# Two heads' scores multiplied in turn, dilated attention by parity, and 22 projection products in halves

## The chip, the cores and the metric

The kernel runs on one core of a Trainium2 chip. The metric is the device time of one execution in microseconds (us), as the median of several runs.

## The reference, cut to what matters

Two stacks of layers over 256 tokens of width 1024, in FP32:

```python
def first_block(x, ...):                      # DEPTH = 2
    x = x + even_mixer(rmsnorm(x), ...)       # 8 stick-breaking heads, 8 NSA heads (2 KV groups)
    x = x + conv_glu_ffn(rmsnorm(x), ...)     # D_FF = 2816
    x = x + odd_mixer(rmsnorm(x), ...)        # 16 forgetting heads: softmax(q k / 8 + c_q - c_k) v
    x = x + conv_glu_ffn(rmsnorm(x), ...)
    return rmsnorm(x)

def second_block(x, ...):
    x = x + 0.5 * swiglu(rms(x));  x = x + hgrn2(rms(x));              x = x + 0.5 * swiglu(rms(x))
    x = x + 0.5 * swiglu(rms(x));  x = x + dilated_attention(rms(x));  x = x + 0.5 * swiglu(rms(x))
```

All heads of the attentions named here have 64 channels. Dilated attention has three groups (window and dilation 128 and 1, 512 and 4, 2048 and 16); a head's result is one softmax over the scores of the three groups, each with a bias by distance. NSA heads attend to compressed, selected and window keys; with 256 tokens the last two see all keys up to the query's own.

## The kernel before

The activations lie transposed in SBUF: channels on the 128 partitions in 8 chunks, 256 tokens along the free side (`x`, and its split into two FP32R parts `xH` and `xL`). Weights come from HBM in pieces of 1 MB (`w`, SP's queue), and ACT and DVE split each into `wH` and `wL` (L276, L277). A projection (`gemm`) makes 2 x 128 output channels for 256 tokens from such a piece: for each of 8 chunks `c` and two halves `j` three products of 256 columns, high by high (L323), then L326 and L327, 48 in all, accumulated in one PSUM bank (`ps_mm`). The products of the feed-forward output (L295 to L297) are of the same kind.

`gemm` has an argument `cut`: the first product of chunk 1 is then issued in several column pieces, with the same weights. Before, only feed-forward blocks use it: each of the six blocks (f0, f1, s00, s01, s10, s11) has five cut gate projections, at m = 4, 8, 12, 16 and 20, each block with the five patterns of `CUTS` in another rotation (L120). A block projects (0, g) and (0, u), computes the norm, which has a small product `ps_sm<-acc,ones` on PE, and goes on with (2, g), (2, u), (4, g) and so on. In s01 and s10 some extra work (bias table, a transpose) follows m = 8.

Attention heads lie in pairs: one 128-partition tile of `qT` and one of `kT` hold head a = 0 in partitions 0 to 63 and head a = 1 in partitions 64 to 127. Score products are FP32 with 64 contracted partitions and write to banks named `S` (two in the even mixer and the forgetting attention, three in the dilated attention); `mm` at L334 issues them and all other small products. DVE adds mask or bias and takes the maximum (L578, L580, L1340, L1344), ACT takes the exponent, PE transposes (L605, L1357), ACT copies, and PE multiplies with the values into `o`. In detail:

- `scores` (even and forgetting): one head and one bank a call. 128 late queries by 256 keys, then 128 early queries by 128 keys; in the forgetting attention each of the two is followed by an `extra` FP32R product that adds the decay (`CF`, `sel`).
- NSA `weigh(j, a)`: one head, both branches (selected, window); `mix(j, a)` multiplies with the values. `compressed` issues 16 products of 15 columns, in the order pair j, head a, query half tt.
- Forgetting `weigh`: head 0 in full, then head 1 in full.
- Dilated `weigh(u, G, bias, j, a, sm)`: one head, both parities t of the queries. Tokens stand with even and odd ones apart. Bank S0 takes group 0 of both parities (256 columns each), S1 groups 1 and 2 (128 columns each); DVE reads a half of a bank behind the products that fill it.

The order of the program is written by hand in strings (EVD, FXD, HGD, DLD; in DLD `q`, `k`, `v` are projections, `n` norms of heads, `t` their transposes, `w` a `weigh`, `m` a `mix`, and the digits are group of heads u, then g, or j and a). A list scheduler then orders each engine's instructions by that order and by what is ready, so projection products can stand between those of heads. PE works through its list in order.

Of the kernel before, what the change touches and what calls it, by code (L numbers as in the profile page):

```python
# [97 lines left out]
def _layout(parts):  # L98
    off, at = {}, 0
    for n, w in parts:  # L100
# [98 lines left out]
class Net:  # L199
# [106 lines left out]
    def gemm(self, out, W, by_token=False, X=None, w0=0, chunks=None, cut=None):  # L306
# [6 lines left out]
        for c in range(c0, c1):  # L313
            for j in range(2):
# [223 lines left out]
    def wout(self, tag, oH, oL, done):  # L538
# [18 lines left out]
    def scores(self, q, k, extra=None):  # L557

        S = self.psum((P, 384), "S")
        self.mm(S[:, 0:256], q[:, 128:256], k, stop=extra is None)  # L560
        if extra is not None:
            extra(S[:, 0:256], 256)
        self.mm(S[:, 256:384], q[:, 0:128], k[:, 0:128], stop=extra is None)
        if extra is not None:
            extra(S[:, 256:384], 128)
        return S

# [71 lines left out]
    def even(self, done):  # L639
        nc, tc = self.nc, self.tc  # L640
        with ExitStack() as ctx:
# [124 lines left out]
            def compressed(qr, kc, gview):  # L766

                Sc = [self.psum((P, 2, 4, 32), "S") for _ in range(2)]
                for j in range(4):
                    for a in range(2):  # L770
                        rows = slice(64 * a, 64 * a + 64)
                        for tt in range(2):
# [37 lines left out]
            def weigh(j, a):  # L810
                rows = slice(64 * a, 64 * a + 64)
                q = qr[j // 2][rows, j % 2, :]
                Sl = [self.scores(q, kkr[rows, b, :]) for b in range(2)]
                h = j + 4 * a
# [4 lines left out]
                nc.vector.tensor_mul(rs[:], rs[:], gview[:, :, h, 1:3])  # L819
                for b in range(2):  # L820
                    for tt in range(2):
                        v = ABs[b][1 - tt]
                        nc.vector.tensor_scalar(v, v, rs[:, tt, b:b + 1], None, ALU.mult)
                NS[j, a] = ABs

            def mix(j, a):
                if a == 0:
                    NO[0] = self.psum((P, 2, P), "o")
                o, ABs = NO[0], NS.pop((j, a))
                for b in range(2):  # L830
                    PT = self.transpose_p(ABs[b])
                    s = slice(128 * b + 64 * a, 128 * b + 64 * a + 64)
                    self.pv(o[:, :, 64 * a:64 * a + 64], vs[:, 0, s], vs[:, 1, s], PT, a + b == 0)
                if a == 0:
# [111 lines left out]
    def fox(self, done):  # L946
        nc, tc = self.nc, self.tc
        with ExitStack() as ctx:
# [40 lines left out]
            def weigh(u, j, qT, kT, e):  # L989
                Sl = []  # L990
                for a in range(2):
                    rows = slice(64 * a, 64 * a + 64)
                    h = 4 * u + 2 * j + a

                    def extra(S, n, h=h, rows=rows):
                        self.mm(S, sel[rows, h:h + 1].to_broadcast([64, P]), CF[rows, 0:n], start=False)
                    Sl.append(self.scores(qT[rows, j, :], kT[rows, j, :], extra))
# [248 lines left out]
    def dilated(self, kH, kL, Rkv, done):  # L1246
        nc, tc = self.nc, self.tc
        with ExitStack() as ctx:
# [9 lines left out]
            def project(u, g, n):  # L1258
                o = self.psum((P, 2, T))
                W = self.w("dl", n, u, g)  # L1260
                self.gemm(o, W, True, None if n == "q" else (kH, kL))
# [64 lines left out]
            def weigh(u, G, bias, j, a, sm):  # L1326
                rows = slice(64 * a, 64 * a + 64)
                hl = 2 * j + a
                q, k = ([G[g][i] for g in range(3)] for i in range(2))
                q, k = ([z[rows, j, :].rearrange("p (t n) -> p t n", t=2) for z in y] for y in (q, k))  # L1330
                S0, S1 = self.psum((P, 2, T), "S"), self.psum((P, 2, 2, P), "S")
# [264 lines left out]
```

## Time and profile before

| | |
|---|---|
| median of 3 runs | 1860.16 us (1859.75 to 1860.5) |
| profiled execution, its own time | 1861.3 us |
| its span, first to last instruction | 1859.5 us |
| busy: PE, PEld, DVE, ACT, POOL | 1841.7, 1806.4, 1270.9, 1042.1, 3.9 us |
| DMA | 314.72 MB, mean 169 GB/s |

Times in the profile are us from the first instruction. PE are products and transposes, PEld the loads of their stationary operand. Products overlap: the record of a 256-column product lasts some 0.28 us, while the next one starts earlier. The rows of the page and of the trace stand below.

### The profile page before, as it was taken

What the parts mean: (1) busy time and instruction counts of PE and PEld (TensorE: products, weight loads), DVE (VectorE), ACT (ScalarE), POOL (GpSimd) and SP (SyncE); (2) the same over time, 40 slices, a digit from 0 to 9 for tenths busy, and PEclk for the clock granted to TensorE, in tenths of its full rate; (3) what the DMA queues carried; (4) which work ended last, traced back from release to release, by engine and by line L of the source; (5) the groups of instructions that cost most, each with busy time, mean ns of one, the idle gap of its engine ahead of it and who ended that gap; (6) DMA issues with size and microseconds to landing.
All of it is one profiled execution on the core that took longest, in us unless ns stands there. A gap on an engine that the chain in (4) does not pass through costs nothing.

```text
span 1859.5 us, 37851 instructions
## 1 busy us (share of the span) xinstructions
PE 1841.7 (99%) x15729; PEld 1806.4 (97%) x15729; DVE 1270.9 (68%) x2695; ACT 1042.1 (56%) x2167; POOL 3.9 (0%) x18
## 2 busy tenths in 40 slices
PE   8999999999999999999999999999999999999999
PEld 7989999999999999999999999999999999999999
DVE  6557986654888686658998766766666456458763
ACT  5456665454666555546766545645456556556542
POOL 0000000000000000000000000000000000000000
PEclk9999999999999999999999999999999999999999
DMA  7313555531565546554335655555564344325553
GB/s 251 121 37 137 207 202 188 195 138 59 183 225 180 205 165 216 182 194 180 115 104 197 217 193 193 192 192 187 190 225 154 142 137 156 118 91 215 194 185 111
DMA packets 61160, 314.72 MB, mean 169 GB/s; under 512 B 10459, under 2 KB 21115, under 8 KB 28348
## 3 DMA queue, kind: packets, MB, share of 16 engines
q1 hardware_dynamic: 45792, 305.16, 46.5%
q10 hardware_dynamic: 15196, 7.15, 1.5%
q8 instruction: 123, 2.02, 0.4%
q14 instruction: 49, 0.40, 0.1%
HBM read 311.17 MB, written 1.11 MB: 168 GB/s over the span
## 4 chain that ended last, share of the span: by engine, by line
PE 93%; DVE 4%; DMA 2%; ACT 1%; issue 0%; ACTq 0%; SPq 0%
PE ps_mm L323 21%; PE ps_mm L326 21%; PE ps_mm L327 20%; PE ps_mm L297 6%; PE ps_mm L295 6%; PE ps_mm L296 6%; PE ps_S L334 5%; PE ps_o L334 4%; DVE wL L277 1%; DMA raw<-in_wall_dram 1%; PE ps_PT L1357 1%; PE ps_PT L334 1%; PE ps_PT L605 1%; DVE X L1165 0%; PE ps_PT L1302 0%; PE ps_PT L631 0%
## 5 line engine op out<-in xcount | busy, mean ns | idle before, releaser
L276 ACT CAST wH<-raw 128x512 fp32r<-128x512 f32 (+1 forms) x1212 | 651.6, 598 | 502.5 <-PE ps_mm L326 253.0
L277 DVE TENSOR_TENSOR wL<-raw,wH 128x512 fp32r<-128x512 f32 (+1 forms) x1212 | 754.8, 661 | 254.2 <-ACT wH L276 252.8
L323 PE MATMUL ps_mm<-xH,wH 128*128 128x256 f32 (+2 forms) x2602 | 716.0, 278 | 8.9 <-ACT xH L345 6.9
L326 PE MATMUL ps_mm<-xL,wH 128*128 128x256 f32 x2560 | 713.1, 279 | 0.6 <-DVE xL L346 0.3
L327 PE MATMUL ps_mm<-xH,wL 128*128 128x256 f32 x2560 | 712.4, 278 | 0.2 <-DVE wL L277 0.2
L323 PEld LDWEIGHTS ps_mm<-xH,wH 128*128 128x128 f32 x2602 | 487.4, 189 | 10.5 <-ACT xH L345 6.9
L327 PEld LDWEIGHTS ps_mm<-xH,wL 128*128 128x128 f32 x2560 | 482.8, 189 | 1.1 <-DVE wL L277 0.7
L326 PEld LDWEIGHTS ps_mm<-xL,wH 128*128 128x128 f32 x2560 | 482.2, 188 | 1.3 <-DVE xL L346 1.3
L297 PE MATMUL ps_mm<-hH,wL 128*128 128x256 f32 x1056 | 291.5, 276 | 0.0
L295 PE MATMUL ps_mm<-hH,wH 128*128 128x256 f32 x1056 | 291.5, 276 | 0.0
L296 PE MATMUL ps_mm<-hL,wH 128*128 128x256 f32 x1056 | 291.5, 276 | 0.0
L295 PEld LDWEIGHTS ps_mm<-hH,wH 128*128 128x128 f32 x1056 | 198.2, 188 | 0.0
L296 PEld LDWEIGHTS ps_mm<-hL,wH 128*128 128x128 f32 x1056 | 198.2, 188 | 0.0
L297 PEld LDWEIGHTS ps_mm<-hH,wL 128*128 128x128 f32 x1056 | 198.2, 188 | 0.0
L323 PE MATMUL ps_mm<-wH,kH 128*128 128x256 f32 x384 | 107.8, 281 | 0.0
L326 PE MATMUL ps_mm<-wL,kH 128*128 128x256 f32 x384 | 107.3, 280 | 0.0
L327 PE MATMUL ps_mm<-wH,kL 128*128 128x256 f32 x384 | 107.3, 279 | 0.0
L323 PE MATMUL ps_mm<-wH,xH 128*128 128x256 f32 x368 | 104.1, 283 | 0.0
L327 PE MATMUL ps_mm<-wH,xL 128*128 128x256 f32 x368 | 103.5, 281 | 0.0
L326 PE MATMUL ps_mm<-wL,xH 128*128 128x256 f32 x368 | 103.2, 280 | 0.0
L505 DVE TENSOR_TENSOR t<-ps_mm,R 128x512 f32<-128x512 f32 x66 | 45.5, 689 | 76.0 <-PE ps_mm L327 75.8
L323 PE MATMUL ps_mm<-oH,wH 128*128 128x256 f32 x256 | 72.8, 285 | 0.0
(296 smaller groups left out, 2264.5 us busy)
## 6 DMA issues: line engine op xcount, KB each, us to landing
raw<-in_wall_dram SPq DMA_DIRECT2D x254, 1024.0 KB, 4.8
raw<-in_wall_dram SPq DMA_DIRECT2D x40, 768.0 KB, 4.3
raw<-in_wall_dram SPq DMA_DIRECT2D x8, 512.0 KB, 3.3
bt<-scr ACTq DMA_DIRECT2D x8, 258.0 KB, 4.9
bt<-scr ACTq DMA_DIRECT2D x4, 512.0 KB, 6.4
x<-in_xin_dram SPq DMA_DIRECT2D x4, 256.0 KB, 5.6
raw<-in_wall_dram SPq DMA_DIRECT2D x4, 256.0 KB, 5.4
cw<-in_cmpw_dram ACTq DMA_DIRECT2D x1, 1024.0 KB
```

Of the source, the lines that this page charges most:

```text
L276: self.nc.scalar.copy(H[:, s], raw[:, s])
L277: self.nc.vector.tensor_sub(L[:, s], raw[:, s], H[:, s].bitcast(F32))
L295: nc.tensor.matmul(out, A[0], B[0], start=start, stop=False)
L296: nc.tensor.matmul(out, A[0], B[1], start=False, stop=False)
L297: nc.tensor.matmul(out, A[1], B[0], start=False, stop=stop)
L323: nc.tensor.matmul(out[:, j, at:at + n], A[0], B[0][:, at:at + n], start=c == c0 and j == 0, stop=False, **k)
L326: nc.tensor.matmul(out[:, j, :], A[0], B[1], start=False, stop=False, **k)
L327: nc.tensor.matmul(out[:, j, :], A[1], B[0], start=False, stop=c == c1 - 1, **k)
L334: self.nc.tensor.matmul(out, l, r, start=start, stop=stop, **k)
L505: nc.vector.tensor_mul(t2[:], u, Rb)
L605: nc.tensor.transpose(pp[:, i * P:(i + 1) * P], s, self.ident[:])
L1357: nc.tensor.transpose(pp[:, i], Pt[:, t, i * P:(i + 1) * P], self.ident[:])
```

## The change

Three things are edited; inputs, constants, layout of the weights and the number of score products stay.

1. `CUTS` and `CUT_OF` go. `cut` becomes a flag: the first product of the second chunk in two halves of 128 columns. It is set in each feed-forward block for (2, g), and in s01 and s10 for (10, u) too; in `wout` (the output projections of the four mixers) for m = 0; and in the dilated attention for ten projections (k00, q02, v02, q11, q20, q21, k22, k30, k31, v32), chosen by a rule on DLD: head work (`w`, `m`, `t`) came before, with only `n` or `s` between, and another projection, `n` or `s` comes next.
2. `scores` takes both heads of a pair and two banks, and issues the products of head 0 and head 1 in turn. NSA `weigh` and `mix` now go by branch b instead of by head a. In `compressed` the loops over a and tt are exchanged.
3. Dilated `weigh` and `mix` go by parity t instead of by head a: one call takes both heads of a pair for one parity, one bank per head, holding group 0 (256 columns), 1 and 2 (128 each), the products of the two heads in turn; DVE reads behind all six.

```diff
-CUTS = ((128, 128), (240, 16), (192, 64), (64, 64, 64, 64), (16, 240))
-CUT_OF = {t: {4 * (i + 1): CUTS[(i + k) % 5] for i in range(5)}
-          for k, t in enumerate(("f0", "f1", "s00", "s01", "s10", "s11"))}
...
-                for n in cut if cut and c == 1 and j == 0 else (T,):
+                for n in (P, P) if cut and c == c0 + 1 and j == 0 else (T,):
...
-                self.gemm(o, W, cut=CUT_OF[tag].get(m) if n == "g" else None)
+                self.gemm(o, W, cut=(m, n) in ((2, "g"), (10, "u") if extra else None))
...
-            self.gemm(o, W, X=(oH, oL), chunks=(0, k1))
+            self.gemm(o, W, X=(oH, oL), chunks=(0, k1), cut=m == 0)
...
+        S = [self.psum((P, 384), "S") for _ in range(2)]
+        for c, n, t in ((0, 256, slice(128, 256)), (256, 128, slice(0, 128))):
+            for a in range(2):
+                self.mm(S[a][:, c:c + n], q[a][:, t], k[a][:, 0:n], stop=extra is None)
+            for a in range(2):
+                if extra is not None:
+                    extra(a, S[a][:, c:c + n], n)
...
-            def weigh(j, a):
+            def weigh(j, b):
+                rows = [slice(64 * a, 64 * a + 64) for a in range(2)]
+                Sl = self.scores([qr[j // 2][r, j % 2, :] for r in rows], [kkr[r, b, :] for r in rows])
...
-                nc.vector.tensor_mul(rs[:], rs[:], gview[:, :, h, 1:3])
+                nc.vector.tensor_mul(rs[:], rs[:], gview[:, :, j::4, 1 + b])
...
-            def weigh(u, G, bias, j, a, sm):
+            def weigh(u, G, bias, j, t, sm):
+                S = [self.psum((P, 512), "S") for _ in range(2)]
+                for g, c, n in ((0, 0, 256), (1, 256, P), (2, 384, P)):
+                    for a in range(2):
+                        q, k = (G[g][i][64 * a:64 * a + 64, j, :] for i in range(2))
+                        self.mm(S[a][:, c:c + n], q[:, t * P:t * P + P], k if g == 0 else k[:, t * P:t * P + P])
...
+                for a in range(2):
+                    b0, b1 = bias[0][:, 2 * j + a, :], bias[1][:, 2 * j + a]
...
+                    for i, m in enumerate((m0, b1)):
+                        c = slice(256 * i, 256 * i + 256)
+                        nc.vector.tensor_tensor_reduce(two(Pt[:, a, c]), two(S[a][:, c]), m, 1.0, 2 * BIG, ALU.add,
+                                                       ALU.max, mx[:, a, i:i + 1])
...
+                cut = heads and its[min(i + 1, len(its) - 1)][0] in "qkvns"
+                heads = n in "wmt" or heads and n in "ns"
```

## Rows read from the trace of the kernel before

**Rows 1.** The page: the first row of part 1 (busy time of each engine, its share of the span, instructions), the row of the granted clock in part 2 (40 equal slices, in tenths), and the first row of part 4 (shares of the chain that ended last).

```profile
PE 1841.7 (99%) x15729; PEld 1806.4 (97%) x15729; DVE 1270.9 (68%) x2695; ACT 1042.1 (56%) x2167; POOL 3.9 (0%) x18
...
PEclk9999999999999999999999999999999999999999
...
PE 93%; DVE 4%; DMA 2%; ACT 1%; issue 0%; ACTq 0%; SPq 0%
```

**Rows 2.** Busy time in two stretches of 30 us in one feed-forward block, where the PE row of the timeline shows products of a projection alone. Columns: the stretch in us from the span's start, its length, then for PE, PEld, DVE, ACT and POOL the busy time and (x) the instructions that touch the stretch, the granted clock, the share of the DMA engines and GB/s. A product lasts 0.28 us by the profile and overlaps the next, so the spacing is (length + 0.28) / count.

```profile
676.00:706.00 30.00, 30.00 (x257) 30.00 (x256) 28.28 (x56) 17.99 (x33) 0.00 (x0) 1.00 0.51 184
...
711.00:741.00 30.00, 30.00 (x267) 30.00 (x266) 20.61 (x34) 14.32 (x27) 0.00 (x0) 1.00 0.50 178
```

**Rows 3.** Timeline of PE at four of the products that the kernel already does in pieces: start and length in us, engine, line, operation, names, shape, count. 194 us: two halves. 260 us: four quarters. 687 us: 192 and 64 columns. 1199 us: 16 and 240.

```profile
194.01 0.33 PE L323 MATMUL ps_mm<-xH,wH 128*128 128x128 f32 x2
...
194.35 0.28 PE L327 MATMUL ps_mm<-xH,wL 128*128 128x256 f32 x1
...
259.65 0.53 PE L323 MATMUL ps_mm<-xH,wH 128*128 128x64 f32 x4
...
260.22 0.28 PE L327 MATMUL ps_mm<-xH,wL 128*128 128x256 f32 x1
...
686.93 0.31 PE L323 MATMUL ps_mm<-xH,wH 128*128 128x192 f32 x2
...
1198.88 0.39 PE L323 MATMUL ps_mm<-xH,wH 128*128 128x16 f32 x2
```

**Rows 4.** Busy time in stretches of projections, columns as in rows 2. The first five lie in four feed-forward blocks (183: f0, 1002: s01, 1186 and 1223: s10, 1684: s11), the last three in the dilated attention.

```profile
183.00:193.00 10.00, 10.00 (x87) 10.00 (x87) 9.75 (x20) 7.79 (x15) 0.00 (x0) 1.00 0.38 140
...
1002.00:1014.00 12.00, 12.00 (x108) 12.00 (x107) 10.89 (x20) 9.14 (x17) 0.00 (x0) 1.00 0.63 221
...
1186.00:1216.00 30.00, 30.00 (x257) 30.00 (x256) 22.20 (x38) 17.01 (x31) 0.00 (x0) 1.00 0.58 203
...
1223.00:1231.00 8.00, 8.00 (x73) 8.00 (x72) 5.58 (x9) 3.44 (x7) 0.00 (x0) 1.00 0.34 131
...
1684.00:1697.00 13.00, 13.00 (x113) 13.00 (x112) 9.76 (x18) 8.55 (x15) 0.00 (x0) 1.00 0.62 231
...
1398.00:1408.00 10.00, 10.00 (x88) 10.00 (x87) 6.06 (x11) 6.23 (x12) 0.00 (x0) 1.00 0.51 184
...
1452.00:1482.00 30.00, 30.00 (x257) 30.00 (x256) 15.61 (x30) 15.12 (x31) 0.00 (x0) 1.00 0.44 160
...
1484.00:1499.00 15.00, 15.00 (x130) 15.00 (x129) 11.53 (x24) 8.82 (x19) 0.00 (x0) 1.00 0.47 166
```

**Rows 5.** Timeline of PE at two stretches of score products of the dilated attention that stand between other work, each with the row that follows it. [...]

```profile
1427.95 0.70 PE L334 MATMUL ps_S<-k,qT 64*128 64x256 f32 x2
...
1428.58 0.55 PE L334 MATMUL ps_o<-vN,PT 128*128 128x64 f32 x3
...
1436.39 0.71 PE L334 MATMUL ps_S<-k,qT 64*128 64x128 f32 x4
...
1437.02 0.39 PE L327 MATMUL ps_mm<-wH,xL 128*128 128x256 f32 x1
```

**Rows 6.** Timeline of PE in the even mixer where score products of the stick-breaking heads (qT,kT) and of the NSA heads (kkr,nqr) follow one another.

```profile
106.83 0.48 PE L334 MATMUL ps_S<-kkr,nqr 64*128 64x256 f32 x1
...
106.94 0.38 PE L334 MATMUL ps_S<-qT,kT 64*128 64x128 f32 x2
...
107.15 0.38 PE L334 MATMUL ps_S<-kkr,nqr 64*128 64x256 f32 x1
...
107.16 0.27 PE L334 MATMUL ps_S<-qT,kT 64*128 64x128 f32 x1
...
107.37 0.38 PE L334 MATMUL ps_S<-kkr,nqr 64*128 64x128 f32 x2
```

**Rows 7.** Busy time of the instructions that write or read the score banks ps_S alone (columns as in rows 2, POOL left out by the view): the NSA heads of the even mixer with some of the stick-breaking ones, the forgetting attention, the dilated attention.

```profile
105.00:146.00 41.00, 16.81 (x87) 11.80 (x84) 11.40 (x37) 0.98 (x2) 1.00 0.06 21
...
389.00:453.00 64.00, 15.48 (x96) 11.76 (x96) 8.75 (x28) 0.00 (x0) 1.00 0.26 90
...
1421.00:1647.00 226.00, 32.50 (x192) 22.50 (x192) 26.06 (x64) 0.00 (x0) 1.00 0.38 131
```

**Rows 8.** Timeline of PE: the first and the last of the 28 stretches of score products in the dilated attention.

```profile
1421.83 3.19 PE L334 MATMUL ps_S<-k,qT 64*128 64x256 f32 x20
...
1644.84 0.48 PE L334 MATMUL ps_S<-k,qT 64*128 64x128 f32 x2
```

**Rows 9.** Timeline of PE in the forgetting attention: the start of a pair of heads whose products are not interrupted and the row after its end (the rows between are left out), and a first product that stands alone between transposes and value products.

```profile
389.30 0.70 PE L334 MATMUL ps_S<-kT,qT 64*128 64x256 f32 x2
...
390.86 0.39 PE L323 MATMUL ps_mm<-xH,wH 128*128 128x256 f32 x1
...
404.74 0.70 PE L334 MATMUL ps_S<-kT,qT 64*128 64x256 f32 x2
```

**Rows 10.** Timeline of PE: one of the four stretches of score products with the compressed keys (15 columns).

```profile
97.91 1.06 PE L334 MATMUL ps_S<-kcr,nqr 64*128 64x15 f32 x8
```

**Rows 11.** The first head stage of the dilated attention: the reduction that empties half a score bank and the read of its accumulator (groups of instructions: line, engine, operation, names, shapes, count, busy us, mean ns of one, idle us before, releaser), and the busy time of the stage (columns as in rows 2).

```profile
L1340 DVE CUSTOM_DVE_ANT_1 Pt<-ps_S,bt 128x256 f32<-128x256 f32 x8 | 3.3, 421 | 4.7 <-PE ps_S L334 4.2 <-PE ps_PT L1357 0.5
...
L1340 DVE DVE_READ_ACCUMULATOR2_ANT mx<- 128x1 f32 x8 | 0.7, 83 | 0.0
...
1421.00:1450.50 29.50, 29.38 (x233) 26.53 (x232) 16.07 (x60) 19.59 (x43) 0.00 (x0) 1.00 0.35 107
```

More of the change, by code (lines that the diff above doesn't have):

```diff
@@ L304, in gemm_a, with gemm @@
             self.mm3(out, (W[0][:, c, s], W[1][:, c, s]), (XH[:, c, :], XL[:, c, :]), c == 0, c == KC - 1)
-    def gemm(self, out, W, by_token=False, X=None, w0=0, chunks=None, cut=None):
+    def gemm(self, out, W, by_token=False, X=None, w0=0, chunks=None, cut=False):
         nc = self.nc
@@ L769, in compressed @@
                 for j in range(4):
-                    for a in range(2):
-                        rows = slice(64 * a, 64 * a + 64)
-                        for tt in range(2):
+                    for tt in range(2):
+                        for a in range(2):
+                            rows = slice(64 * a, 64 * a + 64)
                             self.mm(Sc[a][:, tt, j, 0:15], qr[j // 2][rows, j % 2, tt * P:(tt + 1) * P], kc[rows, :])
@@ L989, in weigh, with extra @@
             def weigh(u, j, qT, kT, e):
-                Sl = []
-                for a in range(2):
-                    rows = slice(64 * a, 64 * a + 64)
+                rows = [slice(64 * a, 64 * a + 64) for a in range(2)]
+                def extra(a, S, n):
                     h = 4 * u + 2 * j + a
-                    def extra(S, n, h=h, rows=rows):
-                        self.mm(S, sel[rows, h:h + 1].to_broadcast([64, P]), CF[rows, 0:n], start=False)
-                    Sl.append(self.scores(qT[rows, j, :], kT[rows, j, :], extra))
+                    self.mm(S, sel[rows[a], h:h + 1].to_broadcast([64, P]), CF[rows[a], 0:n], start=False)
+                Sl = self.scores([qT[r, j, :] for r in rows], [kT[r, j, :] for r in rows], extra)
                 sm = self.sp.tile([P, 2, 2], F32, name="sm2")
@@ L1256, in dilated, with project @@
             RS = cp.tile([P, 2, 2], F32, name="RS")
-            def project(u, g, n):
+            def project(u, g, n, cut):
                 o = self.psum((P, 2, T))
                 W = self.w("dl", n, u, g)
-                self.gemm(o, W, True, None if n == "q" else (kH, kL))
+                self.gemm(o, W, True, None if n == "q" else (kH, kL), cut=cut)
                 return o
@@ L1324, in biases @@
                 return b0, b1
-            def weigh(u, G, bias, j, a, sm):
[L1327 to L1331, printed above, removed]
-                b0, b1 = bias[0][:, hl, :], bias[1][:, hl]
+            def weigh(u, G, bias, j, t, sm):
+                two = lambda z: z.rearrange("p (b n) -> p b n", b=2)
+                S = [self.psum((P, 512), "S") for _ in range(2)]
+                for g, c, n in ((0, 0, 256), (1, 256, P), (2, 384, P)):
+                    for a in range(2):
+                        q, k = (G[g][i][64 * a:64 * a + 64, j, :] for i in range(2))
+                        self.mm(S[a][:, c:c + n], q[:, t * P:t * P + P], k if g == 0 else k[:, t * P:t * P + P])
@@ L1346, in weigh @@
                 nm = self.sp.tile([P, 2], F32, name="nmj")
                 nc.vector.tensor_reduce(nm[:], mx[:], AX.X, ALU.max, negate=True)
-                for t in range(2):
-                    nc.scalar.activation(Pt[:, t], Pt[:, t], AF.Exp, bias=nm[:, t:t + 1], accum_out=sm[:, t, a:a + 1])
-                return Pt
-            def mix(v, Pt, j, a, o):
-                s = slice((2 * j + a) * 64, (2 * j + a) * 64 + 64)
-                for t in range(2):
+                for a in range(2):
+                    nc.scalar.activation(Pt[:, a], Pt[:, a], AF.Exp, bias=nm[:, a:a + 1], accum_out=sm[:, t, a:a + 1])
@@ L1355, in mix @@
+                return Pt
+            def mix(v, Pt, j, t, o):
+                for a in range(2):
+                    s = slice((2 * j + a) * 64, (2 * j + a) * 64 + 64)
                     pp = self.psum((P, 4, P), "PT")
                     for i in range(4):
-                        nc.tensor.transpose(pp[:, i], Pt[:, t, i * P:(i + 1) * P], self.ident[:])
+                        nc.tensor.transpose(pp[:, i], Pt[:, a, i * P:(i + 1) * P], self.ident[:])
                     PT = ap.tile([P, 4, P], F32, name="PT", bufs=3)
@@ L1364, in dilated @@
             B = {}
-            for it in DLD.split():
+            its, heads = DLD.split(), True
+            for i, it in enumerate(its):
                 n, w = it[0], tuple(int(z) for z in it[1:])
+                cut = heads and its[min(i + 1, len(its) - 1)][0] in "qkvns"
+                heads = n in "wmt" or heads and n in "ns"
                 if n == "q" or n == "k":
-                    B[(n,) + w] = project(*w, n)
+                    B[(n,) + w] = project(*w, n, cut)
                     if it[2:] == "0" and n == "k":
@@ L1371, in dilated @@
                 elif n == "v":
-                    B[("v",) + w] = values(project(*w, n))
+                    B[("v",) + w] = values(project(*w, n, cut))
                 elif n == "s":
```

54 lines of the change are left out of this document (17 added, 37 removed).

## The prediction

> **What bounds the kernel now.** I read the page first. TensorE has work under way for 99% of the span, its clock is granted at the full level in every slice, and 93% of the chain that ended last is PE, nearly all of it the three product lines of the projections [rows 1]. DVE is at 68% and ACT at 56%, so they are covered on average. The kernel ends earlier only if PE's own stream of instructions gets shorter. A busy share of 99% cannot say how fast that stream runs, because products overlap in the record; so the second thing to read is the spacing of product starts. In one block, the same 256-column product starts every (30 + 0.28) / 257 = 0.1178 us in one stretch and every 30.28 / 267 = 0.1134 us in another [rows 2]. Both stretches are busy for all of their 30 us at clock 1.00, so this is no wait and no throttle: there are two paces, 4.4 ns apart, and the reader should see that only the counts differ.
>
> Third, I read what happens at the products that are already cut [rows 3], and which pace holds around them [rows 4]; last the score products of the heads, their spacing alone and beside others [rows 5 to 10], and DVE behind them [rows 11]. The profiled execution took 1861.3 us for a span of 1859.5; the median of the runs is 1860.16, so terms taken from the span can be subtracted from the median as they stand.
>
> **Part 1: the halves.** A cut into two pieces takes from 194.01 to the next-but-one product at 194.35, 0.34 us where two products at the fast pace take 0.227: it costs 0.114. A cut in four takes 0.57 and costs 0.34 [rows 3]. The old list has 30 cut products, five in each of six blocks; in each block four are in two pieces and one in four. Removing them gives 24 x 0.114 + 6 x 0.34 = 4.8 us. The new 22 (six at (2, g), two at (10, u), four in the output projections, ten in the dilated attention) cost 22 x 0.114 = 2.5 us. Net **-2.3 us**.
>
> What a cut does to the pace: before the two halves at 194.01 the pace is 10.28 / 87 = 0.118, and in s10 the slow pace (257 in 30 us) runs through the cut 16 + 240 at 1198.88 and ends at the next one, two halves at 1221.6, behind which 73 in 8 us is 0.1134. The cut 192 + 64 at 686.93 lies inside the slow stretch of rows 2 and changes nothing either [rows 2 to 4]. The third pair of halves that met the slow pace, in s11, also ended it. So two halves set the fast pace in three cases of three, and two other patterns failed once each. I take halves as sure.
>
> Feed-forward: in f0, f1 and s11 the slow pace holds from the small product of the norm to the cut in (4, g), and the new cut in (2, g) lies 96 products earlier: 3 x 96 x 4.4 ns = 1.27 us. In s00 and s10 the first old cut failed, so the new one is 288 products earlier: 2 x 288 x 4.4 ns = 2.53 us. s01 is at 12.28 / 108 = 0.1137 already [rows 4] and gains nothing. Sum **-3.8 us**.
>
> Dilated attention: from 1398 on almost every projection is slow (88 in 10 us, 257 in 30, 130 in 15) [rows 4]. A cut helps to the next interruption, since the transposes and head products set the pace anew. Where the cut projection starts behind transposes and runs undisturbed, the products behind the seventh count: q02 and v02 90 each, q20 and k22 138 each, k30 42, v32 90, together 588 x 4.4 ns = **-2.6 us**. Those of q11, q21 and k31 stand among head products in PE's order of before, and long slow stretches such as the one at 1452 begin behind that head work; I give them nothing, up to 2.3 us if the order changes (518 products). The output projections: 36-product pieces chopped by head work, 0 (0 to 0.3). In the two blocks with extra work, (10, u) stands where the pace is fast already: 0. Part 1 is **-8.7 us**, from -5 (dilated gains nothing) to -11.
>
> **Part 2: scores in turn.** No product is added or removed; the two heads of a pair stand in partitions 0 to 63 and 64 to 127, and the order decides whether neighbours differ in that. Alone, two records of 256 columns take 0.63 us to the next row and four of 128 take 0.63: with 0.216 and 0.112 a record this leaves 0.19 for entering and leaving such a stretch [rows 5]. When the two kinds of heads stand side by side, the trace shows two streams at once: records of kkr at 106.83, 107.15 and 107.37 keep their own spacing while three of qT,kT start between them, one 10 ns behind a kkr record [rows 6]. So adjacent products of different halves run at the same time. The Trainium skill states this too (TensorE: Matmul & The Clock Gate, Part 3, "The mechanism": tiles in different row groups overlap, starting some 4 ns apart); the trace agrees where the two are neighbours, and by its span model every pair would cost one product, the case of rival (a) below.
>
> Price of the pairs. Dilated: each of 16 weighs (4 groups, 2 pairs, 2 parities) issues 2 x (2 x 0.216 + 4 x 0.112) = 1.76 us, paired 0.88. All paired saves 14.1 us. But the records now take 32.5 us busy [rows 7], while 64 x 0.216 + 128 x 0.112 + 28 x (0.19 + 0.07) = 35.5 (0.07 is the modelled tail of each of the 28 stretches [rows 8]); so 3 us overlap already and must be taken off. The second parity of a pair finds one free score bank of three; the other comes free only when DVE has read two halves at 0.50 us each [rows 11]. Meanwhile a scheduler that takes what is ready puts the first head's three products in alone, as it did with lone products in before. I pair all first parities and a quarter of the second, 10 of 16: 8.8 us less most of the 3, that is **-6.5** (-4 to -11).
>
> Forgetting attention: an uninterrupted pair takes 1.56 us [rows 9]; one head by its prices takes 2 x 0.216 + 2 x 0.112 + 0.11 + 0.06 + 0.19 = 1.02, so 0.54 is saved. Three of the eight pairs run like this now, by the timeline: 1.6 us is the low end. If all eight take 1.02 and a tail, 15.48 busy [rows 7] becomes 8.7, 6.8 saved. The others start with a lone product in a hole [rows 9]; I take the middle, **-3.7**. NSA heads: 32 x (0.216 + 0.112) = 10.5 us of records, at best 5.2 saved, nothing if two banks never come free together; **-2.6**. Compressed keys: 32 records of 0.112, eight to a stretch [rows 10]; 1.8 or 0, **-0.9**. Sum -13.7.
>
> What is late next: per weigh, DVE's four reductions take 2.0 us and follow the products; they started between them before, now all of one bank's products come first. In the head stage DVE is busy 16.1 and ACT 19.6 of 29.5 us [rows 11], and projection products stand there to fill holes, so most of it stays covered; I take a tenth off for new waits: **-12.3 us**. Everything else (exponents, transposes, value products, the gates' strided slices) keeps its count and size: nothing.
>
> Sum: 1860.2 - 8.7 - 12.3 = **1839 us**.
>
> **Rivals.** (a) *All pairs meet*: scores -11.1 - 6.8 - 5.2 - 1.8 = -24.9, with the halves 1827. For it: the clean overlap of rows 6. Against: the score banks. (b) *Pairs are torn or eaten*: a bank wait or a filler stands between the two heads nearly everywhere, each extra stretch costs 0.19, or what PE gains it waits for DVE; only the halves count, 1851.5. For it: 28 stretches for 16 weighs now [rows 8]. The Trainium skill has a rule for this (TensorEngine Tiling, "Key Properties": a change of tiling mode drains the engine); the 0.19 of rows 5 agrees. (c) *The halves don't hold*: the pace behind them comes out slow, or head work resets it at once; 2.3 of the 8.7 remain, 1845.5. (d) *Slower*: PE works in order, and the second head's first product now stands ahead of the first head's rest. If in each of the 32 weighs it waits for the bank while DVE reads two halves, 32 x 1.0 = 32 us are lost against 21 gained: 1871. It decides from 0.66 us per weigh. Against: PE is busy for 29.4 of 29.5 us in a head stage [rows 11], so such holes are filled with other products now, and all its idle time is 18 us [rows 1].
>
> **Numbers.** Forecast 0.55, (a) 0.18, (b) 0.15, (c) 0.05, (d) 0.03; 0.04 for gains and waits that cancel. A change of under 0.2% (3.7 us) can't be told from none here. (a), (b), (c) and the forecast are all over it: faster 0.93, same 0.03, slower 0.04. The range takes in (a) and (b), 1826 to 1852; the forecast's own is 1831 to 1846.
>
> **What would show it.** Halves: at most a few cut products at 0.34 us, and behind (2, g) in every block about 267 products in 30 us; in the dilated attention 0.1134 behind q02, v02, q20, k22. Pairs: four 256-column records in some 0.55 us; busy time of ps_S near 26 us instead of 32.5 in the dilated attention, near 12 instead of 15.5 in the forgetting attention. Wrong if ps_S stays near 32 and 15 (b), if PE shows waits on DVE mx of more than 10 us in all (d), or if stretches behind two halves still count 257 (c).

## The result and the profile after

The changed kernel takes **1847.4 us** (1846.3 to 1848.3), the kernel before 1859.95: a ratio of 0.9934, interval 0.9917 to 0.9951, 12.6 us less. A second comparison gave 1849.0 against 1861.0, again 0.9934 (0.992 to 0.9947). The forecast was 1839, with a range of 1826 to 1852 and a narrower one of its own, 1831 to 1846. Sign and wide range held; the narrow range was missed by 1.4 us, and the point was 8 us too low.

The page after, same parts as [rows 1]: TensorE is as full as before, with 20 product records fewer, and the chain is more PE's than before.

```profile
PE 1826.5 (99%) x15709; PEld 1792.6 (97%) x15709; DVE 1268.5 (69%) x2695; ACT 1041.6 (56%) x2167; POOL 3.9 (0%) x18
...
PEclk9999999999999999999999999999999999999999
...
PE 95%; DVE 2%; ACT 1%; DMA 1%; issue 0%; SPq 0%; ACTq 0%
```

Busy time in stretches of projections, columns as in [rows 2]. The first four lie behind the new halves of (2, g) in f0, s00, s10 and s11; the next two behind the halves of q02 and v02 in the dilated attention, then a long stretch behind head work there, then two behind the halves of q20 and k22.

```profile
184.00:214.00 30.00, 30.00 (x267) 30.00 (x267) 26.50 (x49) 19.76 (x36) 0.00 (x0) 1.00 0.55 182
...
672.00:702.00 30.00, 30.00 (x267) 30.00 (x266) 27.70 (x53) 16.99 (x30) 0.00 (x0) 1.00 0.53 187
...
1182.00:1212.00 30.00, 30.00 (x268) 30.00 (x267) 23.01 (x37) 17.62 (x31) 0.00 (x0) 1.00 0.55 194
...
1676.00:1706.00 30.00, 30.00 (x267) 30.00 (x266) 25.04 (x41) 18.83 (x34) 0.00 (x0) 1.00 0.62 222
1390.00:1400.00 10.00, 10.00 (x87) 10.00 (x86) 5.84 (x11) 5.71 (x13) 0.00 (x0) 1.00 0.40 149
1402.00:1411.00 9.00, 9.00 (x78) 9.00 (x78) 6.08 (x10) 5.49 (x12) 0.00 (x0) 1.00 0.52 186
1441.00:1471.00 30.00, 30.00 (x267) 30.00 (x266) 17.20 (x34) 15.93 (x33) 0.00 (x0) 1.00 0.48 176
1475.00:1489.00 14.00, 14.00 (x121) 14.00 (x121) 11.23 (x24) 8.04 (x17) 0.00 (x0) 1.00 0.45 152
1535.00:1549.00 14.00, 14.00 (x121) 14.00 (x120) 10.23 (x22) 9.02 (x19) 0.00 (x0) 1.00 0.45 170
```

The feed-forward blocks count 267 or 268 in 30 us where [rows 2, 4] had 257 before a cut took effect. In f0, s00 and s10 the slow pace held up to the new halves and ended there; in s11 this execution was fast a little ahead of them. In the dilated attention the new halves don't set it: 9.28 / 78 = 0.119 and 14.28 / 121 = 0.118 us a product is the slow pace, behind four cuts. The one fast stretch shown there (1441) begins behind head work and no cut.

Score products. Each leaves two records in the trace (192 records for the 96 products of the dilated attention). First the busy time of ps_S alone, as in [rows 7]: forgetting attention 15.48 to 11.91, dilated attention 32.50 to 28.14.

```profile
387.00:450.00 63.00, 11.91 (x96) 8.39 (x96) 8.37 (x28) 0.00 (x0) 1.00 0.27 93
1412.00:1634.00 222.00, 28.14 (x192) 19.86 (x192) 24.14 (x64) 0.00 (x0) 1.00 0.39 133
```

Then PE's timeline after: a compressed stretch, a forgetting pair and the row behind it, the first weighs of the dilated attention.

```profile
100.21 1.06 PE L332 MATMUL ps_S<-kcr,nqr 64*128 64x15 f32 x8
...
387.93 0.70 PE L332 MATMUL ps_S<-kT,qT 64*128 64x256 f32 x4
388.28 0.47 PE L332 MATMUL ps_S<-CF,selr 64*128 64x256 f32 x2
388.59 0.39 PE L332 MATMUL ps_S<-kT,qT 64*128 64x128 f32 x4
388.73 0.31 PE L332 MATMUL ps_S<-CF,selr 64*128 64x128 f32 x2
388.96 0.39 PE L321 MATMUL ps_mm<-xH,wH 128*128 128x256 f32 x1
...
1413.30 2.40 PE L332 MATMUL ps_S<-k,qT 64*128 64x256 f32 x18
1415.64 0.39 PE L321 MATMUL ps_mm<-wH,xH 128*128 128x256 f32 x1
1415.86 0.28 PE L324 MATMUL ps_mm<-wL,xH 128*128 128x256 f32 x1
1416.36 0.89 PE L332 MATMUL ps_S<-k,qT 64*128 64x256 f32 x4 [0.22 <-DVE mx L1338]
```

A forgetting pair takes 388.96 - 387.93 = 1.03 us; it was 1.56 [rows 9]. The compressed stretch is what it was (1.06 us for eight records, [rows 10]). The 18 records at 1413 are the first weigh with its heads in turn (the records of the two heads start 7 ns apart) and, behind it, all of one head's products of the second weigh: they take 2.34 us. The other head's products wait at 1416 for DVE to empty a bank.

What PE waited for, by the view of waits (total us, times, longest):

```profile
PE ps_sm L332 <- DVE rel L1400: 2.3, 1, 2.3
...
PE ps_S L332 <- DVE mx L1338: 1.1, 4, 0.4
PE ps_o L332 <- ACT PT L606: 0.5, 1, 0.5
```

All three are new. The first stands at the start of s01, the others belong to the heads and are small.

### The profile page after: what moved, and what is told of

It reads as the page before. It is cut to its first block, busy times and chain, and to the rows that moved or that the text cites. A ratio compares the mean times of both kernels' runs of the same rounds, so it can differ in the third digit from the quotient of the medians.

```text
span 1846.5 us, 37819 instructions
## 1 busy us (share of the span) xinstructions
PE 1826.5 (99%) x15709; PEld 1792.6 (97%) x15709; DVE 1268.5 (69%) x2695; ACT 1041.6 (56%) x2167; POOL 3.9 (0%) x18
## 4 chain that ended last, share of the span: by engine, by line
PE 95%; DVE 2%; ACT 1%; DMA 1%; issue 0%; SPq 0%; ACTq 0%
PE ps_mm L321 21%; PE ps_mm L324 21%; PE ps_mm L325 21%; PE ps_mm L293 6%; PE ps_mm L292 6%; PE ps_mm L294 6%; PE ps_S L332 4%; PE ps_o L332 4%; DMA raw<-in_wall_dram 1%; PE ps_PT L1351 1%; DVE wL L274 1%; PE ps_PT L332 1%; PE ps_PT L604 0%; PE ps_PT L1298 0%; ACT wH L273 0%; PE ps_PT L630 0%
## 5 line engine op out<-in xcount | busy, mean ns | idle before, releaser
L321 PE MATMUL ps_mm<-xH,wH 128*128 128x256 f32 x2568 | 713.1, 278 | 8.8 <-ACT xH L343 7.0
L321 PE MATMUL ps_mm<-wH,kH 128*128 128x256 f32 (+1 forms) x390 | 108.1, 279 | 0.0
L321 PE MATMUL ps_mm<-wH,xH 128*128 128x256 f32 (+1 forms) x372 | 104.2, 282 | 0.0
L321 PEld LDWEIGHTS ps_mm<-wH,kH 128*128 128x128 f32 x390 | 72.9, 188 | 0.0
```

## The experiments

**The halves alone.** The kernel before with the new cuts and its old heads:

```diff
-    for n in cut if cut and c == 1 and j == 0 else (T,):
+    for n in (P, P) if cut and c == c0 + 1 and j == 0 else (T,):
...
```

> The kernel before with the 22 halves in place of its 30 old cuts, scores and order of heads as before. Theory: halves set the fast pace only where the weights are stationary (feed-forward, output projections); in the dilated attention, where the activations are stationary, they only cost 0.114 us each. Feed-forward -8.5 us, dilated +1.1: 1852.5 us, and behind q02, v02, q20, k22, k30, v32 the spacing stays 0.1177 before and after the cut. Rival (the prediction's step): the halves also act in the dilated attention, another -2.6 and more: 1849, spacing 0.1133 behind these cuts.

Measured: 1856.6 against 1860.1, ratio 0.9982 (0.9973 to 0.9991): 3.5 us, less than either theory. Part of it is the clock at the opening (below): at a granted clock of 0.999 over the span the two executions took 1854.5 and 1854.7, those of the kernel before 1860.1 to 1861.6. In the profiles the opening up to the NSA scores is 2.6 us longer than before. The six feed-forward blocks are together 6.7 us shorter, where the theory had 8.5; s01 gains nothing, because PE waits 1.4 us there (the last experiments show for what). In the dilated attention the stretches that begin with a half-cut projection or behind head work count as before:

```profile
1450.00:1480.00 30.00, 30.00 (x257) 30.00 (x256) 15.62 (x30) 15.11 (x31) 0.00 (x0) 1.00 0.47 159
1483.00:1497.00 14.00, 14.00 (x121) 14.00 (x120) 11.19 (x24) 8.00 (x17) 0.00 (x0) 1.00 0.50 160
```

The dilated stage with its output projection takes 316.7 us, against 315.8 before: ten cuts are paid for and nothing comes back. Rival (c) of the prediction, that halves don't hold, is true for this stage and false for the feed-forward.

**The scores alone.** The changed kernel with the old list of 30 cuts.

> The changed kernel with the 30 old cuts in place of the 22 halves, so the new order of scores alone. Theory: the score products give 10 us of PE (2.5 NSA, 3.4 forgetting, 4.2 dilated), waits for the score banks take about 1.5 back: 1851.5 us, or 1849.5 if the long stretch of projections behind the first head stage of the dilated attention comes out at the fast pace again without any halves. Rival: half of what PE gains is lost to new waits: 1855.

Measured: 1852.6, ratio 0.9954 (0.9939 to 0.9969), 7.5 us. The two parts alone add up to 11.0, the whole is 12.6 and, measured again below, 12.0: no large interaction.

**No cut at all.**

```diff
-    self.gemm(o, W, cut=CUT_OF[tag].get(m) if n == "g" else None)
+    self.gemm(o, W)
```

> The kernel before with no product cut. Theory: a pace holds until something interrupts the products; without a cut the five feed-forward blocks that start slow stay slow to their end, some 1500 products each: +29 us for the pace, -4.8 for the cuts saved: 1884 us. Rival: the pace comes right by itself within a block: 1855 us.

Measured: 1881.6 (1873.8 to 1886.0), ratio 1.0107 (1.008 to 1.0133). The pace lasts until something ends it. Stretches of f0, s00 and f1 without a cut:

```profile
185.00:215.00 30.00, 30.00 (x257) 30.00 (x256) 27.17 (x50) 20.44 (x37) 0.00 (x0) 1.00 0.51 185
760.00:790.00 30.00, 30.00 (x257) 30.00 (x256) 21.01 (x35) 15.26 (x30) 0.00 (x0) 1.00 0.50 178
500.00:530.00 30.00, 30.00 (x267) 30.00 (x266) 27.03 (x50) 20.34 (x37) 0.00 (x0) 1.00 0.55 201
```

f0 and s00 are slow here, f1 is fast. In this execution f0, s00 and s11 stay slow to their ends, the output included (62.07 us instead of 59.73); s10 is fast behind the extra work that follows m = 8, s01 and f1 without a cut. f1 was slow up to the small product of the norm and fast behind it, so such a product can change the pace too.

**A bank of its own for each head.** In the dilated attention head 0 takes the single bank of one name, head 1 one of two of another, and the six products are chained in turn (the lines of the chain are left out here):

```diff
-    self.banks(ctx, mm=2, S=3, PT=2, o=1)
+    self.banks(ctx, mm=2, S=1, Sb=2, PT=2, o=1)
...
-    S = [self.psum((P, 512), "S") for _ in range(2)]
+    S = [self.psum((P, 512), "S"), self.psum((P, 512), "Sb")]
...
```

> The changed kernel; in the dilated attention head 0 of a pair always takes one bank of its own and head 1 the other two in turn, and the six products are tied in order, so that none starts before the bank that comes free last. Theory: the score banks tear the pairs (head 0's three products go ahead alone); now 12 of 16 calls have all their products side by side: busy time of ps_S in the dilated attention falls from some 28.7 us to 24, the median by 3 to 4 us, to 1843.5. Rival: the pairs meet, but PE then waits for DVE or ACT instead: ps_S falls, the time stays at 1846 to 1848.

Measured: 1851.9 (1848.1 to 1855.5), ratio 0.9958 (0.9941 to 0.9975): no gain. From the first record of each stretch to the start of what follows, summed over the stage by the timeline, score products took 31.2 us before, 27.0 in the changed kernel and 24.3 here: in twelve of the sixteen weighs the two heads now run side by side. But the stage as a whole takes 317.1 us instead of 312.7. PE's waits in it are now:

```profile
PE ps_PT L1357 <- ACT Pt L1349: 1.8, 5, 0.4
PE ps_S L1330 <- DVE mx L1344: 1.6, 3, 0.7
```

3.4 us against 1.1. Projection products are also slow more often: of the starts in the stage 1327 followed at the slow pace instead of 917, 410 x 4.4 ns = 1.8 us. These two make 4.1 of the 7.1 us that were lost beside the scores (4.4 more for the stage, 2.7 less for the scores). The other 3 us are not located; projection products now break the score stretches more often, 33 stretches instead of 24. Banks and chain came in one edit, so what each of them did is not separated.

**The changed kernel again.**

> The changed kernel unaltered, beside the next two. The first comparison gave 0.9934 (12.6 us less). If the gain is the sum of the two parts run alone (3.5 us for the halves, 7.5 us for the scores), its ratio comes out at 0.994 or a little above, 11 us less; if the two help each other, as a forecast of 21 us had it, it is 0.992 or less. At the same granted clock the halves alone were 5.5 us ahead of the kernel before, so 13 us are expected at the same granted clock.

Measured: 0.9934 (0.992 to 0.9947), 12.0 us: the sum of the parts within what can be told.

**No halves in the dilated attention.**

```diff
-    self.gemm(o, W, True, None if n == "q" else (kH, kL), cut=cut)
+    self.gemm(o, W, True, None if n == "q" else (kH, kL))
```

> The changed kernel, but the ten projections of the dilated stage are not cut. Theory: with the activations as the stationary operand the halves set no pace, they only cost 0.113 us each, so this kernel is 1.1 us faster than the changed one (0.0006 of the time), and the stretches at q02, v02, q20, k22, k30 and v32 count at 0.1178 us per product in both. Rival: the halves are what let the three long fast stretches of the dilated stage come about (558 products of 4.4 ns, 2.5 us), so leaving them out costs 2.5 - 1.1 = 1.4 us.

Measured: 1846.0, ratio 0.9916 (0.9903 to 0.993); beside it the changed kernel had 1849.0. The dilated stage is 1.06 us shorter than in the first profile of the changed kernel (311.6 against 312.7), as the theory has it, but only 0.4 us shorter than in the second, where the stretch behind k22 came out fast. The rival is half right: the stretches at 1516 and 1641, fast with the halves in both profiles, are slow without them (1198 slow starts against 917 and some 780). (With the same halves, but none in the output projections, the second of them is slow again.) At 4.4 ns a start that is worth 1.2 to 1.9 us, and ten cuts cost 1.1, so by these two sums the halves should win; about 1 us more is lost with them, and it is not located. The remaining 2 us of the medians are not in the stage. Part may be the wait at the start of s01, 1.5 us here and 2.3 in the changed kernel, and part the clock, 0.998 in four of five executions of the changed kernel and in one of four of this one.

**Other patterns.** Three cuts in each projection of the dilated attention, 19 patterns.

```diff
+PATS = ((F, H, F), (Q, F, F), (F, F, H), ((240, 16), F, F), ((64, 192), F, F), (F, Q, F),
...
```

> The changed kernel, with three cuts in each of the 24 projections of the dilated stage, at the second, fourth and sixth block of 128 rows, in 19 patterns: halves, quarters, 240 and 16, 16 and 240, 192 and 64, 64 and 192 columns, of the first, the second or the third product of a block. Theory: with the activations stationary no cut of the moving weights sets the pace: stretches that begin at 0.1178 us stay there behind all or nearly all of the cuts. Rival: it is only the pattern (halves of the first product) that fails there, and some others bring 0.1134 us behind each of their cuts, as the halves do in the feed-forward. Each of the 72 cuts costs 0.11 us or more, so the whole kernel is some 7 us slower than the changed one unless the pace is set.

Measured once: 1864.7, span 1862.9, for 72 cuts. By the starts just ahead of each cut and just behind it, halves of the second product ended a slow pace at 2 of 3 places, 64 and 192 columns of the second at 1 of 2, 240 and 16 of the second at 3 of 6 and of the first at 2 of 4, halves of the first at 1 of 3, halves of all three at 1 of 6, and the other thirteen patterns at none. Where the pace was fast, halves or 64 and 192 of the second kept it at 3 of 3 each, while four pieces and 64, 64, 128 columns of the first turned it into the slow one in six cases of six. So a cut sets the pace for better or worse, and the theory that no cut does so with stationary activations is wrong.

**The second product cut instead of the first.** Nine cuts in the dilated stage, in two kernels, one with 64 and 192 columns, one with halves (P, P) in their place:

```diff
...
-    nc.tensor.matmul(out[:, j, :], A[0], B[1], start=False, stop=False, **k)
+    for n in (64, 192) if here and by_token else (T,):
+        nc.tensor.matmul(out[:, j, at:at + n], A[0], B[1][:, at:at + n], start=False, stop=False, **k)
+        at += n
...
```

> The changed kernel with the ten cuts of the dilated stage replaced by nine, of the second product of a block (64 and 192 columns) instead of the first (two halves), in q02, v02, k11, q20, k21, k22, k30, k32 and v32; the stage's output projection has its halves in the second pair of columns, not in the first. Theory (the pattern decides, and 64 and 192 of the second product bring 0.1133 us behind a slow stretch, as the one such place of the run before showed): the long stretches of the dilated stage run at 0.1133 us; against the kernel with no cut there, 1018 products gain 4.4 ns, 4.5 us, less nine cuts at 0.113, so 3.5 us less: 1842.5, a ratio of 0.990. Rival (the pace behind a cut is an accident of the place): about half of the stretches, a gain of 1 us and less: 1845.

> As the run beside it, but the second product of a block is done in two halves of 128. Theory: the same, 1842.5, since the run before had 0.1178 us in front of such halves and 0.1133 behind them. Rival: 1845.

Measured: 1846.7, ratio 0.992 (0.9907 to 0.9934), with 64 and 192; 1844.4, ratio 0.9908 (0.9895 to 0.9922), with halves. Behind q02, q20 and k22, halves of the second product:

```profile
1388.00:1397.00 9.00, 9.00 (x82) 9.00 (x81) 5.63 (x10) 5.20 (x10) 0.00 (x0) 1.00 0.40 151
...
1473.00:1487.00 14.00, 14.00 (x121) 14.00 (x120) 10.94 (x24) 7.76 (x16) 0.00 (x0) 1.00 0.47 156
1533.00:1547.00 14.00, 14.00 (x126) 14.00 (x125) 10.44 (x22) 8.86 (x19) 0.00 (x0) 1.00 0.42 158
```

and the same stretches with no cut in the stage:

```profile
1389.00:1398.00 9.00, 9.00 (x79) 9.00 (x78) 5.05 (x9) 6.27 (x12) 0.00 (x0) 1.00 0.56 205
...
1473.00:1487.00 14.00, 14.00 (x121) 14.00 (x121) 11.52 (x24) 8.99 (x19) 0.00 (x0) 1.00 0.47 167
1533.00:1547.00 14.00, 14.00 (x121) 14.00 (x120) 9.73 (x22) 9.89 (x21) 0.00 (x0) 1.00 0.51 188
```

q02 (79 to 82) and k22 (121 to 126) are fast now, q20 is not. Seven cuts met a slow stretch undisturbed; five of the seven ended it, in either kernel (with 64 and 192 it is k22 and k32 that stay slow, with halves q20 and k32). Halves of the first product did so at 3 of 30 such places (q02, v02, q20, k22, k30 and v32 in each of five executions: the changed kernel twice, the halves alone, a bank for each head, and the first kernel of the next experiment). The mechanism of the theory held at the five places, its sum of 3.5 us did not: the stage with its output projection takes 310.7 and 311.5 us against 311.6 without cuts, since the nine cuts cost 1.0 us and the long stretch behind the first head stage, fast in the kernel without them, came out slow here. (In the kernel with the scores alone, which has no cut in the stage either, it was slow too.)

**No halves in the output projections**, first in the changed kernel, then in the one with halves of the second product:

```diff
-    self.gemm(o, W, X=(oH, oL), chunks=(0, k1), cut=m == 0)
+    self.gemm(o, W, X=(oH, oL), chunks=(0, k1))
```

> The changed kernel without the halves in the four output projections. In the changed kernel PE waits 2.3 us at the start of s01 for the norm's sum of squares on DVE; none of the kernels with whole products there (the one before, the one with the scores alone, the one without any cut) shows that wait, and the four others with the halves do. Theory: the one more instruction per output projection shifts the list that orders DVE, and three pieces of weights are split ahead of each step of the norm's sum; without the halves the wait goes, s01 from the last output projection on takes 123.8 us instead of 125.6, and with four cuts less at 0.113 the kernel is some 2 us faster than the changed one (ratio 0.9923 instead of 0.9934). Rival: the wait belongs to the scores in turn (later heads, later norm); then it stays, and only 0.45 us are gained.

> The kernel with nine cuts of the second product in halves in the dilated stage (0.9908), without the halves in the output projections of the other three mixers. Theory: again some 2 us less, a ratio of 0.9897, which would be the fastest of all. Rival: 0.9906, since only three cuts go.

In the changed kernel DVE splits three pieces of weights just ahead of the norm's sum (acc) at the start of s01 and one or two between its steps; in the order of before none stand just ahead and one between steps. PE stands until the sum is done. In the changed kernel, DVE, and PE's next product:

```profile
987.99 1.90 DVE L274 TENSOR_TENSOR wL<-raw,wH 128x512 fp32r<-128x512 f32 x3
989.79 0.70 DVE L354 TENSOR_TENSOR acc<-acc,sq 128x512 f32<-128x512 f32 x1
990.39 0.70 DVE L274 TENSOR_TENSOR wL<-raw,wH 128x512 fp32r<-128x512 f32 x1
990.99 0.70 DVE L354 TENSOR_TENSOR acc<-acc,sq 128x512 f32<-128x512 f32 x1
991.60 1.30 DVE L274 TENSOR_TENSOR wL<-raw,wH 128x512 fp32r<-128x512 f32 x2
992.80 0.70 DVE L354 TENSOR_TENSOR acc<-acc,sq 128x512 f32<-128x512 f32 x1
...
994.49 0.70 PE L332 MATMUL ps_sm<-acc,ones 128*128 128x256 f32 x2 [2.28 <-DVE rel L1400]
```

in the order of before, DVE:

```profile
996.02 0.87 DVE L346 SCALAR_TENSOR_TENSOR xL<-x,par,xH 128x256 fp32r<-128x256 f32 x2
996.81 0.68 DVE L356 TENSOR_TENSOR acc<-acc,sq 128x512 f32<-128x512 f32 x1
997.41 0.68 DVE L277 TENSOR_TENSOR wL<-raw,wH 128x512 fp32r<-128x512 f32 x1
998.02 0.68 DVE L356 TENSOR_TENSOR acc<-acc,sq 128x512 f32<-128x512 f32 x1
```

and without the halves in the output projections, PE:

```profile
989.59 0.59 PE L332 MATMUL ps_sm<-acc,ones 128*128 128x256 f32 x2
```

Measured: 1845.2, ratio 0.991 (0.989 to 0.993). The wait is gone. All eight executions with halves in the output projections show it, 1.3 to 2.3 us, and none of the six without. And s01 takes 122.9 us from the last output projection to its own first output product, where the changed kernel took 125.6 and 125.8: the theory held, with 2.8 us where 1.8 was expected. The second kernel: 1841.6, ratio 0.990 (0.9875 to 0.9925); one of its six executions, the profiled one, was granted 0.993 of the clock and took 1852.6. Its last head stage of the dilated attention ran at the half level from about 1622 to 1639 us.

> The fastest kernel so far once more, since the profiled execution of its first run fell on a granted clock of 0.993. Five of its six executions lay between 1840.8 and 1844.0; expected is a median of 1841.5 and a ratio of 0.990, 3 us and more under the same kernel with the halves in the other output projections (1844.4) and 6 to 7 under the changed kernel.

Measured: 1843.8 (1841.6 to 1845.9), ratio 0.9905 (0.9889 to 0.9922). That is 2.3 us over what was expected, with two of its executions at a clock of 0.998; whether it beats the kernel with those three halves (1844.4) can't be told. That it is some 5 us under the changed kernel (0.990 and 0.9905 against 0.9934) is well supported, though the intervals touch: apart from the execution at 0.993, all nine of its times (1840.8 to 1845.9) lie under all nine of the changed kernel (1846.3 to 1850.3).

## Why the prediction was right or wrong

In the two profiled executions the span went from 1859.5 to 1846.5, 13.0 us less, where 21 were forecast. The wide range held because it took in two rivals, not because the sum was close. By the timeline, from the first and last products of each stage:

| step of the prediction | forecast, us | measured, us |
|---|---|---|
| s00, s10: five old cuts go, new ones come, 288 products gain the pace | -1.95, -1.84 | -1.97, -1.86 |
| f0, f1, s11: the same with 96 products | -1.10 each | -1.15, -1.51, -0.92 |
| s01: cuts alone | -0.57 | +1.18 |
| score products, dilated | -6.5 | -4.2 |
| forgetting; NSA; compressed | -3.7; -2.6; -0.9 | -3.4; -2.5; 0 |
| dilated pace, less ten cuts | -1.5 | -0.1 (against the scores alone; -0.7 in the second profile) |
| new waits of the heads | +1.4 | +1.6 |
| the first 106 us | 0 | +2.3 |

The measured column adds up to 12.5 of the 13.0 us. The four cuts in the output projections (+0.46 in the forecast) are not listed; three of them lie outside the stages of the table. So somewhat under 1 us is not located.

**Feed-forward: right, block by block.** The prices of a cut (0.114; every undisturbed half-cut after costs 0.113), the paces and the places where they change were read from the trace, and five of six blocks came out within 0.4 us. Two of the small differences are not the cut's doing: f1 came out fast from its start (73 products at 4.4 ns, 0.3 us of its 0.4), and s11 had turned fast 22 products ahead of its halves.

**s01: the step "everything else keeps its count and size: nothing" failed.** Count and size were kept; the order was not. One more instruction in each output projection moved pieces of weights ahead of the norm's sum in DVE's list, and PE waited 2.3 us. The executions without those halves show no such wait.

**Dilated pace: the step "I take halves as sure" failed.** The three cases it rested on all had the weights stationary and the tokens moving. There the step holds: in the eleven executions with halves, those of the first product met the slow pace 47 times in an undisturbed run of projections with stationary weights, and ended it 47 times. In the dilated attention the same loop runs with the two operands exchanged, and there the same cut fails at 27 of 30 places. No run exchanged the operands at one place and left all else, so that this is the cause is argued, not shown. Which product is cut, and in which pieces, also decides there.

The slow starts in the changed kernel fell from 1440 to 917 (some 780 in the second profile), but most of that stands behind head work, not behind cuts: with the old heads and the same halves (the first experiment) they are 1322, with the new heads and no halves in the stage 1198, and with the scores alone, which has none there either, some 1475. Why those stretches start fast or slow is open. Three executions with the nine halves gave the same pace at all seven places, but a place does not always keep its pace: behind k22 the changed kernel counted 121 in its first profile (the fence of the result) and 126 in the same window of its second:

```profile
1535.00:1549.00 14.00, 14.00 (x126) 14.00 (x125) 10.43 (x22) 8.78 (x19) 0.00 (x0) 1.00 0.44 160
```

**Scores: the mechanism was right, one term too large.** Neighbours of different halves run at once, at the price forecast: 1.03 us for a forgetting pair against 1.02. Forgetting and NSA came within 0.3 us, with some luck: the forecast for the forgetting attention called 3.7 the middle of 1.6 and 6.8, which is 4.2, and the half that it took for the NSA heads was a guess between nothing and all. In the dilated attention the prediction named the reason that would tear pairs, the third bank, and PE's order shows just that: in the first weigh of each group the heads alternate, in the second and third one head's products mostly stand ahead of the other's, in the fourth some pairs meet again. I gave ten weighs of sixteen to the pairs; what was gained is two thirds of that. With banks that let more pairs meet, the products did save 6.9 us, about the forecast's sum, but the stage became 4.4 us longer: the rest of -6.5 was not to be had in this way. In the compressed scores the exchange of loops changed nothing: eight records still take 1.06 us. Why is not settled; no run tried it alone.

**The opening.** The order of PE's products up to 106 us is that of before by their names (only the compressed scores exchange heads and halves), yet 2.3 us were lost there, 0.5 of them by 16 us and nearly all the rest between 43 and 55. The windows from 44 to 50 us, in the profiles of before, after, and the kernel with a bank for each head:

```profile
44.00:50.00 6.00, 6.00 (x35) 5.54 (x36) 3.64 (x8) 3.81 (x8) 0.00 (x0) 0.72 0.50 175
```

```profile
44.00:50.00 6.00, 6.00 (x25) 5.36 (x25) 2.56 (x7) 3.23 (x8) 0.00 (x0) 0.50 0.48 175
```

```profile
44.00:50.00 6.00, 6.00 (x47) 5.49 (x46) 3.82 (x9) 4.75 (x11) 0.00 (x0) 1.00 0.47 175
```

The granted clock was at its half level (1.2 GHz) for part of the window, all of it, or none, with no gap between PE's records, and 35, 25 and 47 products touch it. Just ahead of it PE had a run of 32 narrow products, which stands in all three; here in the kernel before:

```profile
40.15 3.65 PE L334 MATMUL ps_PT<-gw,x 128*128 128x24 f32 x32
```

What decides is not shown. The mean clock differs between executions of one kernel too: the kernel before took 1857 to 1861 us at a mean clock of 1.000 and 1863 to 1865 at 0.997. The three runs shown ahead of the prediction could not show that; some 2 us of the distance from 1839 are of this kind, and single runs that differ by as much say nothing. What of it, if anything, belongs to a kernel stays open.

**Rivals.** (a) ended at the banks. (b), where only the halves count, did not come: the scores alone gave 7.5 us, the halves alone 3.5. (d) did not come: four waits for DVE's mx, 1.1 us in all.

## What to carry to other kernels

A pause-free PE can run at two paces, and a small disturbance in its stream sets which; try a trick of that kind with each choice of stationary operand and each product of the group, and read the counts behind every place, in more than one execution, because what ends the slow pace in one loop begins it in another: four pieces of 64 columns of the first product ended it in s00 of the kernel before and began it in the dilated attention. Put products of different partition halves next to each other, but count the banks first: the gain ends where the consumer of a bank comes late. And when an edit adds one instruction to a list-scheduled program, look for new waits far from the edit; here 2.8 us lay at the start of the stage behind it.

## What the runs showed of the hardware that was not expected

- The pace of 256-column products, once 0.1178 us, can last through a whole feed-forward block of some 1,500 products if nothing cuts it: without cuts f0 took 186.6 us and f1, fast, 180.2.
- A cut can also slow the stream: four pieces of 64 columns, or 64, 64 and 128, turned 0.1134 into 0.1178 us in six cases of six where the activations were stationary.
- Halves of the first of three products ended the slow pace at 47 of 47 places with the weights stationary, and at 3 of 30 with the activations stationary; there halves or 64 and 192 columns of the second did at 5 of 7 in each of two kernels. A cut costs 0.113 us either way.
- Behind a run of 24-column products TensorE, with no gap between its records, was granted the half clock for 0 to 6.8 us from about 44 us on, with the same order of products up to there.
